# Attention in two runs of nine key tiles instead of three of six, each run's values right behind its own scores

## The chip, the cores and the metric

One core of one Trainium2 chip runs the whole kernel. The metric is device time in microseconds. PE is TensorE's matmul stream and PEld its weight loads; DVE is VectorE, ACT is ScalarE, POOL is GpSimd, SP is SyncE, which here issues most DMAs.

## The reference

One layer of a transformer-like block over 2048 latent tokens with a prefix of 256 context tokens, in float32. The part that matters here is the attention: 8 query heads of 64, in two groups of four that share a key and value head, each query reading 256 + 2048 = 2304 keys.

```python
def attend(q, k, v):
    s = jnp.einsum('bkgqd,bknd->bkgqn', q, k, preferred_element_type=jnp.float32)
    p = jax.nn.softmax(s, axis=-1).astype(v.dtype)
    return jnp.einsum('bkgqn,bknd->bkgqd', p, v)
...
        k_all = jnp.concatenate([k_c, k_x], axis=2)
        v_all = jnp.concatenate([v_c, v_x], axis=2)
        attn_x = merge_heads(attend_blocked(q_x, k_all, v_all))
        gm_x = gmlp_spatial(jax.nn.gelu(u_x), jax.nn.gelu(vg_x), gm_norm_g[l], gm_ws[l], gm_bs[l])
        x = x + g1 * branch_merge(attn_x, gm_x, ga_x, gb_x, w_br_attn[l], w_br_gm[l], w_out[l])
        h2 = modulate(x, norm2_g[l], sh2, sc2)
        x = x + g2 * sq_relu_mlp(h2, w_ff1[l], w_ff2[l])
```

Before it stand the modulated norm and one input projection; behind it the merge of the two branches and the squared-ReLU MLP.

## The kernel before, in words

The kernel runs its stages one after the other: projection, attention (from about 773 to 1395 us of the profiled span), merge, MLP. Only the attention's order is changed.

The attention is a list of 16 units (`Unit`), four per block of 512 queries; a unit is one pair of heads over 512 queries, and goes over 18 key tiles of 128 keys. All that follows is in `Kern.attend`, which writes out the order by hand: `order()` holds PE's and DVE's instructions of this loop to the order of the program text. ACT, POOL and SP get their order from the framework's scheduler, which also hands out the buffers; the first writes of the buffers of one kind are held to the program's order.

A unit's steps are methods of `Unit`:

- `load` (SP DMA of the unit's queries), `cast` (ACT, the rounded half), `remainder` (DVE, the rest), `queries` (eight transposes on PE, two copies on ACT).
- `maxima` (PE matmul L1736, DVE reductions L1747, the first two of a unit L1742): 18 steps per unit, each with two PSUM buffers and two reductions.
- `reference` (DVE, L1753 and L1754): the maximum over all steps, negated into the query tile. `low_queries` (four transposes, L186, and an ACT copy, L1714) turns it into the shift that a unit's scores subtract.
- `scores(j)` (L1780): eight matmuls into two PSUM buffers, which ACT's two exponentials (L1790) empty into a tile of the kind `p2` (eight buffers) or, for the last two of each group, `t4` (eight buffers, shared with the queries).
- `values(j)` (L1800): the two products with V into the accumulator `o`, opened at tile 0, and the running sum over the tiles' exponentials, on DVE for tiles 2, 4, 8 and 14 (L1820), on POOL for the others (L1823). In the last unit but one DVE also has the last six tiles, in the last unit all of them.
- `leave` (ACT copy L1830 of `o`, and a DMA on ACT's queue), `join` (DVE, L1835, adds the two running sums), `sums` (PE, L1842, and an ACT copy with two DMAs), `inverse` (SP DMAs and a reciprocal on DVE, once per block of queries).

PSUM is one pool of eight buffers of a bank each (`self.psum({"b": 8})`), for scores, maxima, transposes, sums and `o` alike.

The loop goes over each unit's tiles in three groups of six. In a group it puts out the six scores, behind each of them one step of maxima for a later unit (the next unit's in the first two groups, the one after that's in the third), and then the values of the *previous* group, kept in `pend`. So the values of a unit's last six tiles stand behind the first six scores of the next unit.

In the last unit, `br_raw` and `br_weights` (L148 on ACT, L152 on DVE) fetch and split the first weights of the merge; `gate_in` (L954) fetches its gates.

Of the kernel before, what the change touches and what calls it, by code (L numbers as in the profile page):

```python
# [33 lines left out]
NKT = NKEY // P  # L34
# [25 lines left out]
    "late": {"hl": 20, "f4": 12},  # L60
}
SLOTS = {tag: n for tags in POOLS.values() for tag, n in tags.items()}
GROUP = 6
ON_VECTOR = (2, 4, 8, 14)
EARLY = [(0, p) for p in range(7)] + [(kk, 0) for kk in range(1, KC // 2)]
MIDDLE = [(kk, p) for p in (5, 1) for kk in range(1, KC // 2)] + [(1, 6), (KC // 2 - 1, 2)]
# [1 line left out]
FIRST_INPUTS = range(NU - 10, NU - 1)  # L68


class Kern:
    def __init__(self, ctx, tc, I, out):
        self.tc, self.nc, self.I, self.out = tc, tc.nc, I, out
        self.ctx = ctx
        self.uid = 0
        self.tags = {}
        self.pins = []
        self.fixed = []
        self.steady = []
        self.loads = []  # L80
        self.open_pools, self.pool_of = {}, {}
        self.banks = None
# [736 lines left out]

    def attend(self, units, late):  # L820
        begin = self.here()
        pend, self.ready = [], []
        for i, u in enumerate(units):
            at = lambda n: units[n] if 0 <= n < len(units) else None
            nxt, far, old, older = at(i + 1), at(i + 2), at(i - 1), at(i - 2)
            for gi, g in enumerate(range(0, NKT, GROUP)):
                group = range(g, g + GROUP)
                step = nxt if gi < 2 else far
                if not nxt and gi == 0:
                    raws = [self.br_raw(m, self.t2) for m in range(2)]  # L830
                for j in group:
                    u.scores(j)
                    if step:
                        step.maxima(1)
                    if gi == 0 and j == 2 and far:
                        far.load()
                if gi == 2 and nxt:
                    nxt.low_queries()
                if gi == 2 and i in FIRST_INPUTS:
                    next(late, None)  # L840
                for f in pend:
                    f()
                if gi == 1 and far:
                    far.queries()
                if gi == 0 and far:
                    far.cast()
                if gi == 2 and old:
                    old.sums()
                if gi == 0:
                    if older:  # L850
                        older.inverse()
                    if far:
                        far.remainder()
                if gi == 1:
                    if nxt:
                        nxt.reference()
                    if old:
                        old.join()
                if gi == 2 and i in FIRST_INPUTS:
                    next(late, None)  # L860
                if not nxt and gi:
                    self.ready.append(self.br_weights(raws.pop(0), self.t2))
                pend = [lambda u=u, j=j: u.values(j) for j in group]
            pend.append(u.leave)
        for f in pend:
            f()
        units[-2].inverse()
        self.fixed.append(range(begin, self.here()))

# [806 lines left out]
class Unit:  # L1676
    def __init__(self, kern, n):
        self.k, self.nc = kern, kern.nc
        self.b, self.p = divmod(n, NH // 2)
        self.kv = self.p // 2  # L1680
        self.last = n == NU - 1
        self.vector = range(NKT) if self.last else ON_VECTOR
        if n == NU - 2:
            self.vector = ON_VECTOR[:3] + tuple(range(NKT - GROUP, NKT))
        self.pts = {}
        self.acc, self.own = {}, set()
        self.todo = [("ctx", t) for t in (0, 2)]
        self.todo += [(c, t) for t in range(TT) for c in range(1, NB + 1)]
# [77 lines left out]
    def scores(self, j):  # L1766
# [11 lines left out]
        for n, (keys, q) in enumerate(steps):  # L1778
            for h in range(2):
# [3 lines left out]
                )  # L1783
        if j % GROUP < GROUP - 2:
            whole = k.sb("p2", [2, TB])
# [122 lines left out]
```

## Time and profile before

| | |
|---|---|
| median of 3 runs | 2993.59 us (2993.07 to 2994.03) |
| the profiled execution | 2993.09 us, span 2991.3 us |
| granted TensorE clock | 0.999 |
| PE busy over the span | 2965.5 us, 99% |
| POOL busy over the span | 564.9 us, nearly all in the attention |

A row of the chain of waits has a start, a length and what ran; its times are those at which a piece of work could hand on to the next. A row of the timeline has start and length, engine, line, operation, and in brackets the idle time before it with what ended it. In a line `L1800` is line 1800 of the kernel.

### The profile page before, as it was taken

What the parts mean: (1) busy time and instruction counts of PE and PEld (TensorE: products, weight loads), DVE (VectorE), ACT (ScalarE), POOL (GpSimd) and SP (SyncE); (2) the same over time, 40 slices, a digit from 0 to 9 for tenths busy, and PEclk for the clock granted to TensorE, in tenths of its full rate; (3) what the DMA queues carried; (4) which work ended last, traced back from release to release, by engine and by line L of the source; (5) the groups of instructions that cost most, each with busy time, mean ns of one, the idle gap of its engine ahead of it and who ended that gap; (6) DMA issues with size and microseconds to landing.
All of it is one profiled execution on the core that took longest, in us unless ns stands there. A gap on an engine that the chain in (4) does not pass through costs nothing.

```text
span 2991.3 us, 39857 instructions
## 1 busy us (share of the span) xinstructions
PE 2965.5 (99%) x14973; PEld 2301.8 (77%) x14973; DVE 2023.0 (68%) x2999; ACT 1355.5 (45%) x2058; POOL 564.9 (19%) x420
## 2 busy tenths in 40 slices
PE   7999999999999999999999999999999999999999
PEld 5888888887656565655888888888888888888887
DVE  6848567585777778886655698786656766654455
ACT  4443434342555555554322264444554344444433
POOL 0000000000788999990000000000000000000000
PEclk9999999999999999999999999999999999999999
DMA  7464646643100000012766558898676544446665
GB/s 240 121 220 122 222 141 196 181 133 109 36 12 16 12 22 20 25 33 97 242 177 183 154 186 314 310 327 305 225 241 227 183 155 155 155 149 219 208 216 204
DMA packets 330275, 485.53 MB, mean 162 GB/s; under 512 B 28953, under 2 KB 161345, under 8 KB 330082
## 3 DMA queue, kind: packets, MB, share of 16 engines
q1 hardware_dynamic: 326242, 478.40, 48.3%
q10 hardware_dynamic: 3840, 4.59, 0.4%
q8 instruction: 117, 1.92, 0.3%
q14 instruction: 76, 0.62, 0.1%
HBM read 348.56 MB, written 134.35 MB: 161 GB/s over the span
## 4 chain that ended last, share of the span: by engine, by line
PE 97%; DVE 2%; DMA 1%; SPq 0%; issue 0%; ACT 0%; ACTq 0%; DVEq 0%
PE b L1362 13%; PE b L1361 13%; PE b L1360 13%; PE b L180 11%; PE b L182 11%; PE b L181 11%; PE b L1780 9%; PE b L1800 8%; PE b L1736 2%; PE b L186 2%; DMA w<-in_w_mod 1%; PE b L1842 0%; PE b L290 0%; DVE ts L1747 0%; DVE ac L1820 0%; DVE f L1490 0%
## 5 line engine op out<-in xcount | busy, mean ns | idle before, releaser
L1467 DVE TENSOR_TENSOR f<-f,f 128x1024 fp32r<-128x1024 f32 x224 | 264.7, 1222 | 257.1 <-ACT f L1466 254.6
L1747 DVE TENSOR_REDUCE ts<-b 128x1 f32<-128x512 f32 x512 | 311.6, 682 | 105.8 <-PE b L1736 105.8
L1360 PE MATMUL b<-f,f 128*128 128x512 f32 x896 | 349.3, 390 | 0.0
L1361 PE MATMUL b<-f,f 128*128 128x512 f32 x896 | 349.0, 390 | 0.0
L1362 PE MATMUL b<-f,f 128*128 128x512 f32 x896 | 348.7, 389 | 0.0
L1466 ACT CAST f<-f 128x1024 fp32r<-128x1024 f32 x224 | 224.6, 1052 | 263.6 <-PE b L1361 255.4
L1780 PE MATMUL b<-t,t 64*128 64x512 f32 x2304 | 330.9, 400 | 0.0
L1780 PEld LDWEIGHTS b<-t,t 64*128 64x128 f32 x2304 | 226.2, 184 | 69.3 <-issue 26.0
L1823 POOL TENSOR_TENSOR ac<-ac,p 128x512 f32<-128x512 f32 x204 | 269.0, 1353 | 43.4 <-ACT p L1790 43.4
L1823 POOL TENSOR_TENSOR ac<-ac,t 128x512 f32<-128x512 f32 x146 | 233.1, 1626 | 0.0
L1790 ACT ACTIVATE p<-b 128x512 f32<-128x512 f32 x384 | 206.7, 598 | 48.3 <-PE b L1780 41.5
L152 DVE TENSOR_TENSOR w<-w,w 128x1024 fp32r<-128x1024 f32 x120 | 146.8, 1223 | 114.4 <-ACT w L148 76.3
L180 PE MATMUL b<-t,w 128*128 128x512 f32 x512 | 203.2, 397 | 0.4 <-DVE ts L1742 0.3
L182 PE MATMUL b<-t,w 128*128 128x512 f32 x512 | 199.7, 390 | 0.0
L181 PE MATMUL b<-t,w 128*128 128x512 f32 x512 | 199.5, 390 | 0.0
L1361 PEld LDWEIGHTS b<-f,f 128*128 128x128 f32 x896 | 168.2, 188 | 35.9 <-DVE f L1467 1.6
L1360 PEld LDWEIGHTS b<-f,f 128*128 128x128 f32 x896 | 168.2, 188 | 34.8
L1362 PEld LDWEIGHTS b<-f,f 128*128 128x128 f32 x896 | 168.2, 188 | 34.8
L180 PE MATMUL b<-w,t 128*128 128x512 f32 (+1 forms) x528 | 191.5, 363 | 0.2 <-DVE t L150 0.2
L148 ACT CAST w<-w 128x1024 fp32r<-128x1024 f32 x120 | 126.0, 1050 | 145.0 <-DMA w<-in_w_in 108.9
L182 PE MATMUL b<-w,t 128*128 128x512 f32 (+1 forms) x528 | 190.5, 361 | 0.1
L181 PE MATMUL b<-w,t 128*128 128x512 f32 (+1 forms) x528 | 190.1, 360 | 0.0
(261 smaller groups left out, 6120.8 us busy)
## 6 DMA issues: line engine op xcount, KB each, us to landing
w<-in_w_in SPq DMA_DIRECT2D x120, 512.0 KB
ao_d<-f SPq DMA_DIRECT2D x224, 256.0 KB
f<-ao_d SPq DMA_DIRECT2D x112, 512.0 KB
f<-w2o_d SPq DMA_DIRECT2D x112, 512.0 KB
f<-in_w_ff SPq DMA_DIRECT2D x48, 1024.0 KB
w2o_d<-f SPq DMA_DIRECT2D x112, 256.0 KB
md<-in_w_mod SPq DMA_DIRECT2D x32, 512.0 KB
f<-x_d SPq DMA_DIRECT2D x64, 256.0 KB
```

The costliest lines, as they stand in the source:

```text
L180: mm(ps, sh, mh, start=start, stop=False, skip_group_check=skip)
L181: mm(ps, sh, ml, start=False, stop=False, skip_group_check=skip)
L182: mm(ps, sl, mh, start=False, stop=stop, skip_group_check=skip)
L1360: mm(ps, wh, hh, start=start and k == 0, stop=False, skip_group_check=True)
L1361: mm(ps, wh, hl, start=False, stop=False, skip_group_check=True)
L1362: mm(ps, wl, hh, start=False, stop=k == len(w) - 1, skip_group_check=True)
L1466: self.nc.scalar.copy(h, f32(l))
L1467: self.nc.vector.tensor_tensor(out=l, in0=f32(l), in1=f32(h), op=ALU.subtract)
L1747: nc.vector.tensor_reduce(out=self.mx[:, t, h, c : c + 1], in_=ps[h], axis=AX.X, op=ALU.max)
L1780: self.nc.tensor.matmul(ps[h], keys[h], q[rows[h]], start=n == 0, stop=n == len(steps) - 1, skip_group_check=True,)
L1800: nc.tensor.matmul(self.o[h * HD : (h + 1) * HD, :], k.V[c][:, i, self.kv * HD : (self.kv + 1) * HD], pt[h], start=j == 0, stop=j == NKT - 1,)
L1823: nc.gpsimd.tensor_tensor(out=self.acc[e][:, h], in0=old[:, h], in1=pt[h], op=ALU.add)
```

## The change

Groups are nine tiles instead of six, so a unit has two. Each group's values stand right behind its own scores, `pend` is gone, and `leave` stands at the end of its own unit. No maxima stand behind a group's first tile and two steps behind its last, so that a unit still puts out 18. Maxima go to the next unit up to tile 12 and to the one after that from tile 13 on (`AHEAD = 6` stands in for the old group size there, and in the choice of the last unit but one's tiles for DVE). `reference` of the next unit stands behind tile 12's maxima, inside the second group, instead of behind the second group's values. `remainder` stands ahead of the first group's values, `queries` behind them; `join` ahead of the second group's values, `sums` behind them. In the last unit, `br_raw` is put out ahead of the groups, and `br_weights` behind each of the two. The choice between `p2` and `t4` follows the group size: 14 and 4 tiles of a unit instead of 12 and 6.

```diff
--- before.py
+++ after.py
@@ -60,7 +60,8 @@
     "late": {"hl": 20, "f4": 12},
 }
 SLOTS = {tag: n for tags in POOLS.values() for tag, n in tags.items()}
-GROUP = 6
+GROUP = 9
+AHEAD = 6
 ON_VECTOR = (2, 4, 8, 14)
 EARLY = [(0, p) for p in range(7)] + [(kk, 0) for kk in range(1, KC // 2)]
 MIDDLE = [(kk, p) for p in (5, 1) for kk in range(1, KC // 2)] + [(1, 6), (KC // 2 - 1, 2)]
@@ -819,51 +820,46 @@
 
     def attend(self, units, late):
         begin = self.here()
-        pend, self.ready = [], []
+        self.ready = []
         for i, u in enumerate(units):
             at = lambda n: units[n] if 0 <= n < len(units) else None
             nxt, far, old, older = at(i + 1), at(i + 2), at(i - 1), at(i - 2)
+            if not nxt:
+                raws = [self.br_raw(m, self.t2) for m in range(2)]
             for gi, g in enumerate(range(0, NKT, GROUP)):
                 group = range(g, g + GROUP)
-                step = nxt if gi < 2 else far
-                if not nxt and gi == 0:
-                    raws = [self.br_raw(m, self.t2) for m in range(2)]
                 for j in group:
                     u.scores(j)
-                    if step:
-                        step.maxima(1)
-                    if gi == 0 and j == 2 and far:
+                    step = nxt if j <= NKT - AHEAD else far
+                    if step and j > g:
+                        step.maxima(1 if j < group[-1] else 2)
+                    if j == 2 and far:
                         far.load()
-                if gi == 2 and nxt:
+                    if j == NKT - AHEAD and nxt:
+                        nxt.reference()
+                if gi and nxt:
                     nxt.low_queries()
-                if gi == 2 and i in FIRST_INPUTS:
+                if gi and i in FIRST_INPUTS:
                     next(late, None)
-                for f in pend:
-                    f()
-                if gi == 1 and far:
-                    far.queries()
                 if gi == 0 and far:
                     far.cast()
-                if gi == 2 and old:
-                    old.sums()
+                    far.remainder()
+                if gi and old:
+                    old.join()
+                for j in group:
+                    u.values(j)
                 if gi == 0:
+                    if far:
+                        far.queries()
                     if older:
                         older.inverse()
-                    if far:
-                        far.remainder()
-                if gi == 1:
-                    if nxt:
-                        nxt.reference()
-                    if old:
-                        old.join()
-                if gi == 2 and i in FIRST_INPUTS:
+                elif old:
+                    old.sums()
+                if gi and i in FIRST_INPUTS:
                     next(late, None)
-                if not nxt and gi:
+                if not nxt:
                     self.ready.append(self.br_weights(raws.pop(0), self.t2))
-                pend = [lambda u=u, j=j: u.values(j) for j in group]
-            pend.append(u.leave)
-        for f in pend:
-            f()
+            u.leave()
         units[-2].inverse()
         self.fixed.append(range(begin, self.here()))
 
@@ -1681,7 +1677,7 @@
         self.last = n == NU - 1
         self.vector = range(NKT) if self.last else ON_VECTOR
         if n == NU - 2:
-            self.vector = ON_VECTOR[:3] + tuple(range(NKT - GROUP, NKT))
+            self.vector = ON_VECTOR[:3] + tuple(range(NKT - AHEAD, NKT))
         self.pts = {}
         self.acc, self.own = {}, set()
         self.todo = [("ctx", t) for t in (0, 2)]
```

## The prediction

> **What bounds the kernel now.** I read the page first, then the busy time by stretches, then the chain of waits inside the attention stage.
>
> ```profile
> span 2991.3 us, 39857 instructions
> PE 2965.5 (99%) x14973; PEld 2301.8 (77%) x14973; DVE 2023.0 (68%) x2999; ACT 1355.5 (45%) x2058; POOL 564.9 (19%) x420
> 1010.00:1050.00 40.00, 40.00 (x272) 24.10 (x271) 30.53 (x43) 22.41 (x42) 36.03 (x26) 1.00 0.04 12
> ```
>
> The last row is one 40 us stretch of the attention (busy PE, PEld, DVE, ACT, POOL, then granted clock, DMA share, GB/s). PE never rests, POOL is at 36.03 of 40, and DMA does nothing that matters. But a busy PE can still be a PE that waits a tenth of a microsecond here and there, so the chain of waits says more. One whole unit of it (start, length):
>
> ```profile
> 974.60 5.30 PE b L1800 x24
> 979.90 1.02 PE b L186 x8
> 980.92 1.13 PE b L1780 x8
> ...
> 988.28 0.59 PE b L186 x4
> 988.87 5.30 PE b L1800 x24
> 994.17 0.86 PE b L1842 x4
> 995.02 1.13 PE b L1780 x6
> ...
> 997.54 1.13 PE b L1780 x8
> ...
> 1002.37 5.30 PE b L1800 x24
> 1007.67 1.13 PE b L1780 x8
> 1008.80 0.23 PE b L1736 x2
> 1009.03 0.91 PE b L1780 x8
> ...
> 1014.94 1.43 PE b L1800 x5
> ```
>
> From 974.60 to 1014.94 is a unit: 40.34 us. It holds three runs of six score tiles (L1780) with their maxima (L1736), three blocks of values (L1800), transposes (L186) and sums (L1842). Undisturbed, a score tile takes 0.91 and a pair of maxima 0.23. The first tile behind another kind of work takes 1.13, so coming back to scores costs 0.22. A values block takes 5.30, while its pairs of weight loads follow at 0.43, and twelve of those are 5.16: the way in costs 0.14. One turn scores-values-scores thus costs 0.36.
>
> ```profile
> 1110.66 0.14 PEld L1800 LDWEIGHTS b<-p,t 128*64 128x64 f32 x2 [0.29 <-issue]
> 1111.09 0.14 PEld L1800 LDWEIGHTS b<-p,t 128*64 128x64 f32 x2 [0.28 <-issue]
> ```
>
> An undisturbed run of six is 1.13 + 5 x 0.91 + 6 x 0.23 = 7.06. Measured: 7.36 from 980.92, 7.35 from 995.02, 7.27 from 1007.67. The excess (0.30, 0.29, 0.21) is PE waiting for PSUM buffers. In the first two runs the output accumulator `o` holds one of the eight buffers, in the third none. What frees the buffers:
>
> ```profile
> 1130.03 0.39 PE L1736 MATMUL b<-t,t 64*128 64x512 f32 x2
> 1130.45 7.27 DVE L1747 TENSOR_REDUCE ts<-b 128x1 f32<-128x512 f32 x12 [1.99 <-PE b L1736]
> 1139.54 0.18 DVE L1753 TENSOR_REDUCE ts<-ts 128x8 f32<-128x40 f32 x1
> 1139.76 1.02 DVE L1754 TENSOR_SCALAR t<-ts 128x8 f32<-128x8 f32 x1
> 1140.69 1.21 DVE L1835 TENSOR_TENSOR ac<-ac,ac 128x1024 f32<-128x1024 f32 x1
> L1754 DVE TENSOR_SCALAR t<-ts x16: 176/1021/1025, 740.6 to 1341.5; 128x8 f32<-128x8 f32 x16
> 1130.29 4.55 ACT L1790 ACTIVATE p<-b 128x512 f32<-128x512 f32 x8 [0.59 <-PE b L1780]
> ```
>
> Twelve reductions in 7.27 stand back to back at 0.60, so a tile's two maxima cost DVE 1.20, against PE's 0.91 + 0.23 = 1.14. Within a score run DVE is the slower engine. It recovers in the values blocks, where it has little to do. ACT's two exponentials cost 4.55 / 4 = 1.14.
>
> **The change part by part.**
>
> *One turn fewer per unit.* Two runs of nine instead of three of six: -0.36. The work is the same (18 score tiles, 18 pairs of maxima, 36 pairs of values loads). Without any wait, the first half is 1.13 + 8 x 0.91 + 9 x 0.23 = 10.48, values 18 x 0.43 + 0.14 = 7.88, `queries` 1.02: 19.38. The second half is 10.48 + 0.59 + 7.88 + 0.86 = 19.81. Sum 39.19, the floor of a unit, 1.15 under today's.
>
> *Values behind their own scores.* The last exponentials of a run are now needed by that run's values. They are the ninth in order, 8 x 0.86 = 6.9 us behind the first, while ACT is at most one tile (1.14) behind: 0. `o` is now opened behind the first run and closed at the unit's end, so run 0-8 has eight buffers and run 9-17 has seven.
>
> *`reference` moves into the run.* It stood behind a values block, where DVE had time. Now DVE gets it behind tile 12's maxima, with five tiles of the run to go. Its two instructions take 1140.69 - 1139.54 = 1.15, and ten reductions queue behind it, and behind those PE, which needs their buffers. I assume that buffers are handed out in the order they come back, so that with seven in turn, score tile k+2 takes its second buffer from the first maximum of tile k. Time from the run's start: tile 10's maxima start at 1.13 + 0.91 = 2.04, and DVE starts 0.42 later (1130.03 to 1130.45), at 2.46. Three tiles of maxima at 1.20 end at 6.05, `reference` at 7.20. Tile 13's first reduction holds its buffer 0.68 longer (the last of the twelve: 7.27 - 11 x 0.60), to 7.88. PE, undisturbed, starts tile 15 at 6.83: it waits 1.05. From there DVE sets the pace: 0.06 at tile 16, 0.05 at 17, and the transposes of `low_queries` wait until tile 16's second reduction ends at 12.07, where PE alone would be done at 10.48. The stall is 1.59. Ends: 0, if buffers in hand cover it, and 1.15 + 8 x 0.06 + today's 0.3 = 1.9. I take 1.6, as the measured 0.30 and 0.29 with seven buffers show no slack left.
>
> *Small waits that stay.* The eight-buffer run of today loses 0.21 with six tiles; I leave 0.2 in each of the new runs (0 to 0.3). Unit: 39.19 + 1.6 + 0.4 = 41.19, which is +0.85. It holds for the 14 units that still have a unit two ahead: +11.9. The last two have no maxima behind the reference and gain the turn alone: -0.7.
>
> *Moved with it.* `far.load` keeps its place on SP. Its cast stays behind the first run and `remainder` follows it at once, now ahead of the additions of tiles 4 and 8; `join` moves ahead of tile 14's. Three instructions like the join's 1.21 make 3.6, and 7.3 if POOL doubles them. DVE ends the first run's maxima 2.8 after PE (2.46 + 18 x 0.60 against 10.48), so it is free 10 us after the scores, and the next maxima come 10.9 after them (7.88 + 1.02 + 2.04): 0. `queries` goes half a run earlier, `leave` with its ACT DMA half a unit earlier, `inverse` with its two SP DMAs stays in the first half; the sums and their ACT DMAs, and the inputs that `late` fetches on SP, stay at the unit's last values; `br_raw`'s four DMAs on SP stay at the last unit's start, and the first `br_weights` comes one block earlier. Nothing on PE queues behind them: 0. Of the exponentials' buffers, a run now uses seven of the eight `p2`, and four of `t4` a unit instead of six. POOL does 26 additions in 36.03 of 40 us, 1.39 each, and gets no more. The second run's sixteen, from its first exponential at about 21.5, end at 43.7, 2.5 us into the next unit, where nothing wants them: 0, at worst one tile's two, 2.8 us.
>
> *The hand-over to the merge.* Today the last additions on DVE queue behind a weight split that waits for ACT:
>
> ```profile
> 1391.52 1.40 DVE L152 TENSOR_TENSOR t<-t,t 128x512 fp32r<-128x512 f32 x2 [12.58 <-ACT t L148]
> 1395.39 0.50 PE L180 MATMUL b<-in,t 128*128 128x512 f32 x1
> 1399.24 0.34 SPq L954
> 1402.63 4.82 DMA gt<-tb_d
> 1409.34 0.61 DVE bw L152
> 1400.00:1410.00 10.00, 7.54 (x33) 5.49 (x31) 5.64 (x10) 2.38 (x4) 0.00 (x0) 1.00 0.97 322
> 1410.00:1420.00 10.00, 10.00 (x35) 7.17 (x36) 5.99 (x10) 3.98 (x8) 0.00 (x0) 0.83 0.96 316
> ```
>
> The gate loads (L954) leave 3.9 after PE has begun the merge, PE rests 2.5 of the ten microseconds from 1400, and in the next ten its granted clock is 0.83, which is 1.7 us of work lost. In the new order the last values, with their additions, come ahead of that split, so the loads can leave about 3 us sooner. What that brings lies between 0 (the loads are late still) and -4.2 (the rest and the clock). I take -2.5, the rest alone.
>
> *Sum:* 2993.1 + 11.9 - 0.7 - 2.5 = 3001.8; the median stands 0.5 above the profiled execution: 3002.
>
> **Rules of the Trainium skill weighed.** The rows price a turn at 0.22 + 0.14. The Trainium skill, "TensorEngine Tiling (Array Packing)", Key Properties, says that a change of tiling mode drains TensorE, without a figure; if the drain were longer than these rows show, the sum would fall, as in the fourth rival. The rows set 1.20 of reductions against 1.14 of matmuls a tile. The same page of the Trainium skill, PSUM Bottleneck, says that tiling speeds up TensorE but not the emptying of PSUM, which may then be the bound. This rule speaks against longer runs, and the trace agrees within a run; if it held to a run's very end, the sum would be the fifth rival's.
>
> **The rivals.**
> 1. *Forecast*: the reference stalls PE. 2996 to 3009.
> 2. *The other side: the buffers in hand cover it.* If DVE may lag 1.2 us before a matmul waits, only the drift stays (8 x 0.06 = 0.5): a unit of 39.19 + 0.5 + 0.2 = 39.89, -0.45 x 14 - 0.7 - 2.5: 2984. For it: the run without `o` waited less. Against it: 0.3 lost in six tiles on a drift of 5 x 0.06. It decides at tile 15's start: 1.14 behind tile 14's, or 2.2.
> 3. *The reference is short.* L1754 has taken 176 ns once; then it costs 0.4 instead of 1.15: 0.75 x 14 less, 2991. Against it: the median of 1021, and POOL, if that is what slows it, is 90% busy here too.
> 4. *A turn costs more than the chain shows*: a matmul's whole length (0.39, the L1736 row) each way, 0.78 instead of 0.36. Then 0.42 x 16 less: 2995. Against it: the chain has no other place for it.
> 5. *PE waits for every reduction of the run*: 2.46 + 18 x 0.60 + 1.15 = 14.4 instead of 12.07, 2.3 more in 14 units: 3034. A wait of 2.8 for an exponential's buffer behind POOL would cost much the same: 3041. Against it: nothing behind the last maxima but one transpose needs a buffer.
>
> **How the numbers follow.** Chances 0.58, 0.18, 0.11, 0.05, 0.08. The first is likeliest, so 3002; its own range is 2996 to 3009. The range for all, 2983 to 3009, leaves out the fifth and the low end of the second. A measurement here tells about 0.2%, 6 us, from no change. Slower (above 2999.6): seven tenths of the first and all of the fifth, 0.49. Faster (below 2987.6): the second, a little of the third and of the first, 0.22. Same: 0.29.
>
> **What would show it.** Right: in the chain, tiles 15 and 16 of a run 9-17 about 1 us longer, and the transposes behind it late; PE waiting for DVE's maxima, which it hardly does now; units of 41.2; the gates' loads right behind the last sums. Wrong: units under 40, PE idle for ACT instead of DVE, or POOL as the releaser.

## The result and the profile after

| | before | after |
|---|---|---|
| median of six runs each, side by side | 2993.78 us (2992.81 to 2997.19) | 3008.22 us (3005.06 to 3008.59) |
| the profiled execution | 2993.09 us, span 2991.3 | 3005.14 us, span 3003.4 |

The ratio is 1.0044 (95% interval 1.0034 to 1.0053): the change makes the kernel slower, and the interval lies wholly above 1. The forecast was 3002 us, with 2983 to 3009 as its range; the median is 6 us above the one and 0.8 under the end of the other. Two of the six executions after took 3005.1 us, four 3008.1 to 3008.6 (three of these at a mean granted clock of 0.999 instead of 1.000); the trace is of one of the two, so all that follows explains +12.05 us.

The page of after, its busy times and the chain's shares by engine:

```profile
PE 2970.5 (99%) x14973; PEld 2300.0 (77%) x14973; DVE 2028.4 (68%) x2999; ACT 1349.3 (45%) x2058; POOL 551.5 (18%) x420
...
PE 93%; DVE 5%; DMA 1%; ACT 0%; issue 0%; SPq 0%; ACTq 0%; DVEq 0%
```

PE still looks 99% busy: a matmul of the scores is recorded with 0.39 us (median, in before as in after), and the next pair starts 0.23 behind it, so that a wait of 0.2 or 0.3 leaves no gap. The chain tells more: DVE's share of it was 2% before and is 5% now. The chain through one unit of after, from the fifth tile of its first run (1009.04) to the last transposes (L1776 is a score tile, L1732 maxima, L1743 and L1738 their reductions, L1749 and L1750 the reference, L187 transposes, L1796 values):

```profile
1009.04 1.26 PE b L1776 x8
...
1015.52 7.88 PE b L1796 x36
1023.39 1.02 PE b L187 x8
1024.42 2.04 PE b L1776 x16
...
1027.85 1.10 PE b L1776 x8
1028.95 0.28 PE b L1732 x2
1029.23 1.29 DVE ts L1743 x2
...
1030.54 0.21 DVE ts L1749
...
1030.77 0.69 DVE t L1750
1031.45 2.38 DVE ts L1738 x4
1033.84 2.40 DVE ts L1743 x4
...
1036.28 0.66 PE b L187 x4
```

From tile 12's maxima (1028.95) to the transposes (1036.28) the chain leaves PE and runs through DVE: reductions, the reference, eight more reductions. Nothing like it stands in the steady units of before. The weight loads' waits in after, from 774 to 1340 us (waited for, total us, times, longest):

```profile
PEld b L1776 <- DVE ts L1738: 10.9, 28, 0.6
PEld b L1776 <- ACT p L1786: 10.5, 39, 0.3
PEld b L187 <- DVE ts L1743: 5.8, 14, 0.4
```

Scores wait 10.9 us for reductions. In before, the same view has no reduction as a releaser, and 9.8 us of scores for ACT. The transposes' waits of 0.4 are mostly not new: in before they are 14 as well, 5.1 us in all, put down to exponentials.

A steady unit of after, by the starts of its matmuls: run 0-8 11.10, values 7.88, transposes 1.02, run 9-17 11.94, transposes 0.59, values 7.78, sums 0.96, together 41.27. Unit by unit against before: the first 0, the second +0.51, the third to fourteenth +10.80 (0.90 each), the last but one +1.22, the last -0.20. With -0.10 at the start that is +12.2; merge and MLP end it at +12.05.

### The profile page after: what moved, and what is told of

Its sections match the earlier page's. It is cut to its first block, busy times and chain, and to the rows that moved or that the text cites. A ratio compares the mean times of both kernels' runs of the same rounds, so it can differ in the third digit from the quotient of the medians.

```text
span 3003.4 us, 39903 instructions
## 1 busy us (share of the span) xinstructions
PE 2970.5 (99%) x14973; PEld 2300.0 (77%) x14973; DVE 2028.4 (68%) x2999; ACT 1349.3 (45%) x2058; POOL 551.5 (18%) x420
## 4 chain that ended last, share of the span: by engine, by line
PE 93%; DVE 5%; DMA 1%; ACT 0%; issue 0%; SPq 0%; ACTq 0%; DVEq 0%
PE b L1357 13%; PE b L1358 13%; PE b L1356 13%; PE b L181 11%; PE b L183 11%; PE b L182 11%; PE b L1796 8%; PE b L1776 7%; PE b L187 2%; DVE ts L1743 2%; PE b L1732 2%; DVE ts L1738 1%; DMA w<-in_w_mod 1%; PE b L1838 0%; PE b L291 0%
## 5 line engine op out<-in xcount | busy, mean ns | idle before, releaser
L1743 DVE TENSOR_REDUCE ts<-b 128x1 f32<-128x512 f32 x512 | 313.3, 679 | 144.9 <-PE b L1732 143.2
L1819 POOL TENSOR_TENSOR ac<-ac,p 128x512 f32<-128x512 f32 x264 | 354.7, 1387 | 71.6 <-ACT p L1786 71.6
L1462 ACT CAST f<-f 128x1024 fp32r<-128x1024 f32 x224 | 224.6, 1052 | 264.0 <-PE b L1357 258.7
L1776 PE MATMUL b<-t,t 64*128 64x512 f32 x2304 | 334.7, 400 | 4.7 <-DVE ts L1738 3.6
L1776 PEld LDWEIGHTS b<-t,t 64*128 64x128 f32 x2304 | 232.0, 184 | 77.4 <-issue 16.3
L1786 ACT ACTIVATE p<-b 128x512 f32<-128x512 f32 x448 | 235.9, 609 | 52.0 <-PE b L1776 39.5
L1796 PE MATMUL b<-p,t 128*64 128x512 f32 x896 | 199.3, 596 | 0.0
```

Of the source, the lines that this page charges most:

```text
L1743: nc.vector.tensor_reduce(out=self.mx[:, t, h, c : c + 1], in_=ps[h], axis=AX.X, op=ALU.max)
L1776: self.nc.tensor.matmul(ps[h], keys[h], q[rows[h]], start=n == 0, stop=n == len(steps) - 1, skip_group_check=True,)
L1786: self.nc.scalar.activation(pt[h], ps[h], AF.Exp)
L1796: nc.tensor.matmul(self.o[h * HD : (h + 1) * HD, :], k.V[c][:, i, self.kv * HD : (self.kv + 1) * HD], pt[h], start=j == 0, stop=j == NKT - 1,)
L1819: nc.gpsimd.tensor_tensor(out=self.acc[e][:, h], in0=old[:, h], in1=pt[h], op=ALU.add)
```

## The experiments

Each kernel ran beside the kernel before, whose median was 2993.7 to 2994.2 us each time. Lengths of runs are from the matmuls' starts, as above.

**Where the time in run 9-17 goes.** The reference out of the run, the reference twice, and the reference in the run of the kernel *before*.

The first takes all 18 maxima of a unit from the unit ahead of it, so that the reference can stand behind the first run:

```diff
-                    step = nxt if j <= NKT - AHEAD else far
+                    step = nxt if j < GROUP else far
...
-                    if j == NKT - AHEAD and nxt:
-                        nxt.reference()
...
                     far.remainder()
+                if gi == 0 and nxt:
+                    nxt.reference()
                 if gi and old:
                     old.join()
```

(Three more steps of maxima stand ahead of the loop, for the first unit.)

> The changed kernel with the reference back in a values block: the next unit's maxima end with the first run (nine there, nine in the second run before), and its reference stands behind the first run's scores, ahead of the first values. Theory (the reference inside the run holds DVE, and PE waits for the buffers behind it): the second run's excess over 10.48 falls from 1.4 to about 0.5, a unit from 41.3 to 40.3, the total by 13 us to about 2993 to 2995, that of the kernel before. Rival A (DVE is too slow for nine tiles with seven buffers wherever the reference stands): the total falls by 3 us at most. Rival B (the values behind their own scores cost the time): no fall at all.

Measured: 3015.33 us, ratio 1.0076 (1.0063 to 1.0088). Run 9-17 fell as the theory said, 11.94 to 11.09, but the kernel became slower. The trace is of the slowest of its five executions, 3022.2 us. In five units the values before the sums took 11.3 to 11.9 instead of 7.78, and the next run up to 12.7. The waits of PE and of its weight loads from 774 to 1420 us, and the join's line (duration ns: least, median, most):

```profile
PE b L1839 <- DVE ac L1832: 18.1, 5, 4.0
PEld b L1839 <- DVE ac L1832: 22.5, 5, 4.9
L1832 DVE TENSOR_TENSOR ac<-ac,ac x15: 1210/2246/9606, 831.0 to 1402.5; 128x1024 f32<-128x1024 f32 x15
```

The sums wait for the join, an addition on DVE that usually takes 1.2 to 2.3 us and takes 9.6 in three of the five units; in the other two it stands behind the scaling of a merge input (L896), which took 9.07 instead of 0.68. What held them is the subject of a later group.

The pauses cost more than themselves: behind four of the five, PE's granted clock is 0.50 for 3.41 or 6.83 us, and there the next run takes 11.8 to 12.7, against 11.05 behind the fifth.

The second:

```diff
     def reference(self):
+        for _ in range(2):
             nm = self.k.small([TT, 2])
             self.nc.vector.tensor_reduce(out=nm, in_=self.mx, axis=AX.X, op=ALU.max)
             self.nc.vector.tensor_scalar(
```

> The changed kernel with every reference done twice, the second time with the same result. Theory: DVE is held 0.9 us more in a run in which PE has nothing left to spare, so all of it shows: +0.9 in 14 units, +12 us, about 3020. Rival A: DVE may lag before a matmul waits, so less than half of it shows, +6 us at most. Rival B: +0.

Measured: 3029.56 us, ratio 1.0119 (1.0105 to 1.0133). Run 9-17 went from 11.94 to 13.16, +1.22. The chain in one of them:

```profile
1038.12 0.70 DVE t L1751
1038.82 0.10 DVE ts L1750
...
1038.95 1.10 DVE t L1751
1040.04 2.38 DVE ts L1738 x4
```

The second pair takes 1038.82 to 1040.04, 1.22 us, and PE loses 1.22: what DVE does more at this place, PE pays in full. Over 14 units that is 17 us, and the profiled execution, 3024.22 us, is 19.1 above after's; 3020 was expected, since a reference was counted at 0.9.

The third leaves the kernel before as it is, but for the place of the reference:

```diff
+                    if j == 14 and nxt:
+                        nxt.reference()
...
                 if gi == 1:
-                    if nxt:
-                        nxt.reference()
                     if old:
```

> The kernel before with one part of the change alone: the reference inside the third run of six, behind its third tile's maxima. Theory: that run, with seven buffers, goes from 0.3 over 7.06 to between 1.1 and 1.6 over, so +0.8 to +1.3 in 15 units: 3006 to 3013. Rival A (only runs of nine are too long for DVE): within 3 us of the kernel before. Rival B (values and scores): the same as the kernel before.

Measured: 3011.49 us, ratio 1.0059 (1.0045 to 1.0073). The third run went from 7.36 to 8.65 in nearly every unit. The reference takes 1.47 us of the chain there (its second instruction has a median of 1.33), and PE loses 1.29 of it. So moving the reference alone, with groups of six and the old order of the values, costs about as much as the whole change (the intervals of the two ratios overlap).

**Two steps of maxima behind the last tile.** One step behind each tile instead:

```diff
-                    if step and j > g:
-                        step.maxima(1 if j < group[-1] else 2)
+                    if step:
+                        step.maxima(1)
```

> The changed kernel with one step of maxima behind every tile of a run, the first and the last too. Theory (what counts is when DVE has done the run's eighteen reductions and the reference): DVE starts one tile earlier but has the same work behind tile 12, so the second run gets 0.1 to 0.3 shorter, in all 1 to 5 us less than the changed kernel: 3003 to 3007. Rival A (two steps behind the last tile are what delays the transposes): 0.4 and more a unit, 6 us or more less.

Measured: 2999.15 us, ratio 1.0019 (1.001 to 1.0028). Run 9-17 took 11.48 instead of 11.94, the rival's size, not the theory's. But only half of it lies where the rival put it. By the matmuls' starts, tile 17 up to the transposes takes 1.51 instead of 1.96, of which 0.23 is the step that now stands elsewhere; the other half is at tile 15, which takes 1.49 instead of 1.69: DVE begins the run's reductions a tile earlier there. I had taken the order of the steps to be nearly free.

**What lengthens run 0-8.** `leave`, which the change put behind the sums, back ahead of them, directly behind the values:

```diff
                 for j in group:
                     u.values(j)
+                if gi:
+                    u.leave()
...
-            u.leave()
```

> The changed kernel with leave ahead of the sums of the unit before, so that ACT copies the output accumulator while PE does the sums. Theory (the first run of a unit loses 0.3 at its fifth tile since ACT begins its exponentials only behind two copies and three DMA issues): -0.3 in 14 units, -4 us, about 3004. Rival (that wait is DVE's, as in the second run): no change.

Measured: 3002.03 us, ratio 1.0033 (1.002 to 1.0046); its profiled execution took 3001.34, 3.8 under after's. Run 0-8 went from 11.10 to 10.82, which makes 3.9 us over 14 units. ACT at the start of a unit: first after, then before, then this kernel (start, length, instruction).

```profile
1045.74 0.58 ACT L1844 COPY t<-b 128x512 f32<-128x512 f32 x1 [7.67 <-PE b L1838]
1046.23 0.59 ACT L1826 COPY t<-b 128x512 f32<-128x512 f32 x1
1046.36 0.53 ACTq L1847 DMA_DIRECT2D sm_d<-t  x2
1046.98 0.35 ACTq L1827 DMA_DIRECT2D at_d<-t  x1
1047.43 7.48 ACT L1786 ACTIVATE p<-b 128x512 f32<-128x512 f32 x14 [0.61 <-DMA sm_d<-t]
```

```profile
995.10 0.59 ACT L1848 COPY t<-b 128x512 f32<-128x512 f32 x1 [4.94 <-PE b L1842]
995.72 0.53 ACTq L1851 DMA_DIRECT2D sm_d<-t  x2
996.35 3.23 ACT L1790 ACTIVATE p<-b 128x512 f32<-128x512 f32 x6 [0.66 <-PE b L1780]
```

```profile
1044.33 0.59 ACT L1845 COPY t<-b 128x512 f32<-128x512 f32 x1 [0.42 <-PE b L1839]
1044.94 0.57 ACTq L1848 DMA_DIRECT2D sm_d<-t  x2
1045.62 6.39 ACT L1787 ACTIVATE p<-b 128x512 f32<-128x512 f32 x12 [0.71 <-POOL ac L1820]
```

(The last view ends at 1052, hence its twelve.) From the start of the sums' copy to the first exponential is 1.69 us in after, 1.25 in before, 1.29 here. In after the copy of `o` and its DMA stand between the two; ACT then runs fourteen exponentials back to back (7.48), and PE waits at its fifth tile (the chain's 1.26 at 1009.04, where 0.91 is undisturbed) for the buffers that they free late. From start to start that tile takes 1.47 us in after and 1.22 here; the others stay.

Both repairs in one kernel, with no other edit:

> The changed kernel with one step of maxima behind each tile and leave ahead of the sums; the reference stays inside the run. The two parts gave 9 and 6 us each and touch different runs: 2993 to 2997, the kernel before or 2 us more.

Measured: 2994.51 us, ratio 1.0007 (0.9998 to 1.0016), runs of 10.77 and 11.49. The two add up, and the change with them is level with the kernel before.

**Values behind their own scores, alone.** The kernel before with its groups of six, but each group's values behind its own scores, and `leave` at the unit's end:

```diff
-                for f in pend:
-                    f()
+                for j in group:
+                    u.values(j)
...
-                pend = [lambda u=u, j=j: u.values(j) for j in group]
-            pend.append(u.leave)
-        for f in pend:
-            f()
+            u.leave()
```

> The kernel before, groups of six and all the rest as it was, with each group's values right behind its own scores and leave at the unit's end. Theory (the order of the values costs nothing by itself): within 4 us of the kernel before; the runs of tiles 6 to 11 now have seven buffers instead of eight and lose 0.1 a unit. Rival B (values behind their own scores wait for their exponentials, or POOL's additions come too late): 8 us or more slower.

Measured: 2996.94 us, ratio 1.0011 (1.0002 to 1.0019). The first run of a unit went from 7.35 to 7.60, the second from 7.26 to 7.37; the rest stayed. The values wait no longer for exponentials than before (5.1 us in 14 waits of their weight loads, against 5.0 in 14). The 0.25 falls at the first run's third tile, which takes 1.44 instead of 1.16: its weight load waits 0.41 us for a reduction, 5.4 us in 13 units. The exponentials of that run begin late too, 1.68 behind the start of the sums' copy; which of the two costs the time, the runs don't show. The second run now has `o` open and one buffer fewer.

**The additions that are held.** The reference out of the run and `leave` ahead of the sums, together:

> Both mends together: the reference behind the first run, and leave ahead of the sums. Each run had its own effect (second run 11.94 to 11.09, first run 11.10 to 10.82), so a unit of 40.15 is expected, and 2993 to 2995 if no addition on DVE is held for 9 us by POOL as it was in the kernel with the first mend alone. If those holds come again in some units, 5 us each: 3000 to 3015. Rival (the mends are worth nothing, the holds are what the reference's place causes): above 3010.

Measured: 3038.97 us, ratio 1.0143 (1.0121 to 1.0165), the slowest of all, and far above both of the expected times. Where nothing is held the runs are what was meant, 10.80 and 11.09, but eight of fifteen joins take 9.6 us, and a ninth stands behind a scaling that takes 9.07. PE waits 31.1 us for these nine, and behind each its granted clock is 0.50 for 3.41 or 6.83 us, 41 us in all; at half the clock that costs, by estimate, about 20 more. One of the eight on DVE's timeline, and POOL's at the same time:

```profile
1054.79 9.63 DVE L1833 TENSOR_TENSOR ac<-ac,ac 128x1024 f32<-128x1024 f32 x1
```

```profile
1043.47 14.96 POOL L1821 TENSOR_TENSOR ac<-ac,p 128x512 f32<-128x512 f32 x12 [5.94 <-ACT p L1788]
1058.36 4.96 POOL L1821 TENSOR_TENSOR ac<-ac,t 128x512 f32<-128x512 f32 x4
```

POOL adds sixteen times without a pause, one each 1.24 us, until 1063.32; the join, begun at 1054.79, ends at 1064.42, 1.1 later, about its own undisturbed 1.2. It looks as if it had got nowhere until POOL paused. If so, a shorter row on POOL must shorten the hold by as much. Next, the same kernel with four of POOL's additions of a unit taken to DVE:

```diff
-ON_VECTOR = (2, 4, 8, 14)
+ON_VECTOR = (2, 4, 8, 11, 14, 16)
```

> The kernel with the reference behind the first run and leave ahead of the sums, in which the join was held for 9.6 us in nine units and the sums waited (3039), with the additions of tiles 11 and 16 on DVE instead of POOL. Theory: POOL's row ends four additions of 1.23 sooner, the held joins take about 4.7, and as sums come 8 us behind the join's start, none waits: units of 40.15, 2990 to 2998. Rival (a hold of its own length): joins of 9.6 and sums that wait, above 3015.

Measured: 2990.22 us, ratio 0.9987 (0.9979 to 0.9996). The join's line in it:

```profile
L1833 DVE TENSOR_TENSOR ac<-ac,ac x15: 1211/4712/4722, 831.2 to 1371.8; 128x1024 f32<-128x1024 f32 x15
```

The longest is 4.72 instead of 9.63; four additions of 1.23 are 4.92. PE no longer waits for a join, its granted clock stays at 1.00 through the attention, and the kernel is 49 us faster than the one that differs from it in this line alone.

The other way out is to have the join elsewhere, behind the first values, where nothing waits for it soon:

```diff
-                if gi and old:
-                    old.join()
...
                     if older:
                         older.inverse()
+                    if old:
+                        old.join()
```

> Both mends, and the join of the unit before moved from the second values block to the end of the first, by when POOL has worked off its first run's additions. Theory (a DVE addition that meets POOL's additions in an unbroken row is held until the row ends): the join is 1.2 to 2.4 us in all units, no sums wait for it, units of 40.15 and 2988 to 2994. Rival (the join is slow for another reason, such as what it waits for): the 9 us joins come again and sums wait.

Measured: 2996.94 us, ratio 1.0006 (0.9998 to 1.0015); 2988 to 2994 was expected. The hold went to the next two-input additions on DVE: in nine units to tile 14's (up to 9.69 us, with no one waiting), and twice to the scaling of a merge input (L897, 9.13), behind which the next run took 15.2 and 15.4 instead of 10.8.

With one step of maxima per tile added to that:

> The reference behind the first run, leave ahead of the sums, the join in the first block, and one step of maxima behind each tile. From the kernel without the last part: its second run of 11.10 shortens by what one step behind each tile was worth with the reference inside the run (0.46), or by less, since nothing holds DVE in the run any more: 10.8 to 11.1. A unit of 39.9 to 40.15, 2987 to 2995.

Measured: 2988.35 us, ratio 0.9981 (0.9972 to 0.999). This beats both kernels: 5.8 us under before, 19.9 under after. Runs 10.79 and 11.08, no two-input instruction of DVE in the attention above 4.2 us. In that place one step per tile shortens no run (11.10 to 11.08); it only shifts when DVE's additions begin. Why they escape the hold there, the runs don't show. With tile 11's additions on DVE as well, meant to show the hold's length:

> The same with tile 11's addition on DVE instead of POOL. Theory (the 9.6 us that a DVE addition is held are the rest of POOL's row of additions): POOL's row in the second half is two additions of 1.23 shorter, so the held additions take 7.2 instead of 9.6, none reaches into the next run, and the scatter of the times gets smaller: 2986 to 2992. Rival (the hold has a length of its own): still 9.6, and times as without this.

Measured: 2988.77 us, ratio 0.9981 (0.9973 to 0.999). Without a 9.6 us hold in either kernel, these two tell nothing about its length.

## Why the prediction was right, and where it was wrong

The sign, the mechanism and the range held, the range by 0.8 us. The sum came out 3.3 us short of the profiled execution: 1.7 in the last two units and 2.3 at the hand-over, less 0.7 that the other fourteen cost less than counted. Its terms came out less well than that.

- **One turn fewer, -0.36.** Right in kind. The last unit, which puts out no maxima, is the place to see it: three runs of 5.68, 5.71 and 5.71 became two of 8.39 where nothing else disturbs them (with `leave` first), and the values lost 0.14: -0.46 a unit. That settles the fourth rival too, which needed 0.78.
- **Values behind their own scores, 0.** Right for the exponentials. What came with the order was not free, as the small waits of run 0-8 show.
- **The stall behind the reference, 1.6, and 0.2 of small waits in that run.** Measured 1.45 for both. The mechanism is shown by the kernel that does it twice and by the one that moves it alone. The reference was shorter than the rows of before gave: 1030.54 to 1031.45, 0.91 instead of 1.15, since L1750 has a median of 690 ns where the old place had 1021. Taken out of the run it gives back 0.85 of these 0.91. The other 0.6 of the 1.45 is left without it, spread over the run's tiles (1.22 each on average instead of 1.14). My walk had 0.05 a tile, as DVE's drift. That it is DVE is not shown: the tiles go at nearly DVE's 1.20, but in the fastest kernel, with the same 0.6, the weight loads' waits that name a releaser end at exponentials (scores alone 16.1 us, 67 times) or at POOL, none at a reduction. Before gave the walk no better ground: 9.8 us of its scores' waits end at ACT, none at a reduction. The walk also put 1.05 of the stall at tile 15's start and 0.43 at the transposes. By the matmuls' starts, tile 15 lasts 1.69 instead of 1.14 (0.55 more), tile 17 up to the transposes 1.96 instead of 1.37 (0.59 more), the others 0.31 together. So the buffers do cover part, but the second rival, in which they cover all, fell. Of the 1.45, one step per tile takes away 0.46: the later start and the two steps at the end were a cost which I didn't price.
- **Small waits in run 0-8, 0.2.** Wrong: 0.62 (11.10 against 10.48). Nearly half of it, 0.28, is `leave`. The step that failed is "Nothing on PE queues behind them: 0": I asked who on PE waits for the output copy and its DMA, and not what is queued behind them on ACT, which is the exponentials that free PE's buffers. The remaining 0.34 lies mostly at the run's end, ahead of the first value; what it is isn't shown.
- **The unit, 41.19.** Measured 41.27, because the reference was too dear by about as much as the small waits were too cheap. The agreement is better than the working.
- **The first two units** were counted with +0.85 each and cost 0 and +0.51.
- **The last two units, -0.7.** Measured +1.0. In the last but one, run 9-17 has no maxima behind the reference, as foreseen, but DVE's next instruction there is the scaling of a merge input, which ACT's rounding waits for, and the exponentials behind that:

```profile
1360.62 1.87 DVE raw L896
...
1362.51 0.02 ACT in L149
...
1363.04 0.60 ACT p L1786
...
1363.68 1.19 PE b L1776 x7
```

  PE's next score starts at 1363.68, behind that chain; the run takes 11.19, and 8.39 in the kernel with tiles 11 and 16 on DVE and neither reference nor maxima in the run.
- **The hand-over, -2.5.** Wrong: -0.2 by the end. The gate loads did leave earlier, ahead of the merge instead of behind its start. The rest on PE stayed, since a later gate load is now the late one: it is issued when DVE has freed a gate buffer, and takes 5.37.

```profile
1404.38 0.34 SPq L950 DMA_DIRECT2D gt<-tb_d  x1
```

```profile
1414.84 0.70 DVE gt L989
...
1415.56 5.37 DMA gt<-ta_d
...
1422.26 0.50 PE b L183
```

```profile
1410.00:1420.00 10.00, 9.55 (x41) 7.33 (x40) 3.16 (x6) 1.72 (x4) 0.00 (x0) 1.00 0.87 269
1420.00:1430.00 10.00, 7.74 (x33) 5.52 (x34) 7.80 (x13) 3.78 (x7) 0.00 (x0) 1.00 0.80 257
```

  In the windows, PE is busy 9.55 and 7.74 of ten microseconds, at a granted clock of 1.00: the rest of 2.7 us is there, the 0.83 of before is not. Counted from the merge's first matmul, after is 1.64 us ahead at the 80th, 0.93 at the 200th, 0.37 at the 1500th and 0.17 at the last. So what the clock gave was taken back by later waits, which I didn't follow up.
- **Additions on POOL, 0.** Right for after itself. The fifth rival's wait for every reduction (a run of 14.4) fell at 11.94. The third rival, a reference of 0.4, fell at 0.91.

What stays open is the small waits above, and the 3 us by which after's median stands above its profiled execution. No trace of a longer execution shows where they lie.

## What to carry to other kernels

Where two engines run at nearly the same pace through a shared set of buffers (here 1.20 on DVE against 1.14 on PE a tile), an instruction moved into their common stretch cost nearly its whole length here, small as it is (0.85 of 0.91, 1.22 of 1.22, 1.29 of 1.47); look for the stretch in which the engine rests. When a copy or a DMA issue is moved on an engine's queue, ask what stands behind it there and whose buffers that frees, not only who reads its result. And an edit that takes a wait away shifts when everything behind it begins: look at the durations of the instructions that it now overlaps, since a saving of 0.85 a unit was lost here several times over to one addition that took 9.6 us instead of 1.2, and to the lower clock behind the pauses that this made.

## What the runs showed of the hardware

DVE's addition of two operands from SBUF was held for as long as POOL went on adding without a pause: 9.6 us, and 4.72 with four additions of 1.23 fewer in POOL's row. In the traces of the four kernels with such holds (the reference out; `leave` first besides; then tiles 11 and 16 on DVE, or the join early) there are 28 joins and additions of 4.7 to 9.7 us, and every one ends 1.08 us behind the last addition of POOL's row, rows of sixteen and of twelve alike. All 28 had begun 0.07 to 0.12 us behind the start of an addition on POOL; others that began so took only 2.2 to 2.3.

The Trainium skill, "SBUF — State Buffer", SBUF: two separate sides, says that such a DVE instruction and a GpSimd instruction that reads SBUF exclude each other, and that the one that starts first keeps the shared ports for its whole instruction. The trace agrees that DVE is shut out, but not on the length: by that rule one addition on POOL, 1.23 us, would be the longest wait, and the join quoted above sat through about seven of them (1054.79 to 1063.32). Why it doesn't always happen (the same line also took 1.21 and 2.25 us) isn't settled.

PE's granted clock in before, in a window of 2 us of its own (the value ahead of the last two), fell to half behind a rest of 2.41 us:

```profile
1412.00:1414.00 2.00, 2.00 (x6) 1.59 (x5) 0.04 (x1) 1.14 (x2) 0.00 (x0) 0.50 1.07 412
```

In after it stayed at 1.00 through a rest of 2.71, and in the kernel with `leave` first it fell to 0.50 behind a rest of the same 2.71. So the length of one rest didn't decide it. Each of these stretches inside a kernel lasted 3.41 us or 6.83.
